# Solve products of a gated DeltaNet as units in TensorE's order, and VectorE's order at three layer ends

## The chip, the core and the metric

The kernel runs on one core of a Trainium2 chip, as one launch. The metric is the device time of that launch in microseconds (us). Before the change it is 1340.41 us, the median of 3 runs from 1339.39 to 1340.73.

## What is computed

A bidirectional encoder trunk of two layers on 512 tokens of width 1024, all in float32: first a gated DeltaNet mixer (8 heads, in chunks of 64 tokens), then a gated linear attention (GLA) mixer (4 heads), each followed by an MLP of width 4096 with squared ReLU. After each of these four parts stands a LayerNorm of the residual sum.

```python
def reference(x, ...):
    for i in range(DEPTH):                                   # 2
        m = _mixer_gdn(x, ...) if i % 2 == 0 else _mixer_gla(x, ...)
        x = _layernorm(ALPHA * x + m, ln1_g[i], ln1_b[i])
        x = _layernorm(ALPHA * x + _sq_relu_mlp(x, mlp_w1[i], mlp_w2[i]), ln2_g[i], ln2_b[i])

def _gated_delta_chunked(q, k, v, beta, g):                  # one direction, per chunk of 64
    gc = cumsum(g); kb = k * beta
    a_mat = where(strict, (kb @ k.T) * decay_mat, 0.0)
    sol = triangular_solve(a_mat + eye(64), [v * beta, kb * exp(gc)], lower, unit_diagonal)
    ...
```

What the change touches most is the triangular solve: for each head, both directions and all chunks, the inverse of a unit triangular matrix.

## The kernel before

Tokens lie in four tiles of 128 (t0 to t3, buffers xt0 to xt3). Products of float32 are done as three matmuls (lines 122 to 124) on operands split into a high and a low half: ScalarE copies the high half (names with h: wh, xth, ah), VectorE subtracts it for the low half (wl, xtl, al).

**The first mixer** (function `gdn`, class `GdnHead`) is a pipeline over heads. For each step of its loop three heads are in work: one in its recurrence (`recur`, matmuls m1, m2, m3, op), one in its solve (`solve`), one in its projections (`project`, products pjk, pjq, pjv, pjz, 24 matmuls of 512 columns each). In the last two steps pieces of the output product (oa) take the place of the projections.

**The solve** works on U = 8 units: 2 directions (d = 0, 1) x 4 tiles of 128 tokens, each tile holding two chunks. Its steps for one head:

- `ep`: the exponents of the decay, by two matmuls a direction; the second adds the causal mask (`mi`, the mask product, line 1538).
- `a4`: the 4 x 4 diagonal blocks, made on VectorE, d = 0 before d = 1. Three doubling steps (`hp`, line 1556): eight matmuls on four columns, then dc on VectorE.
- five levels s = 4, 8, 16, 32, 64 (`prod`, line 1600). Each level has the product lv<-Dd,ath, then pz made from it on VectorE (s below 32), on ScalarE (s = 32, four copies, line 1614) or on both (s = 64, lines 1628 and 1630), and then the two products lv<-pz,Xd and lv<-Xd,pz, from which VectorE updates Dd and Xd. Each product is eight matmuls u = 0 to 7; u = 0 to 3 are d = 0.
- a last correction (`nw`, lines 1646 and 1668).

**The order on each engine** is made by a scheduler from the instructions as the program traces them: an instruction is put into its engine's queue once the scheduler takes its operands to be ready, and a later one can overtake it. Two means of the kernel steer it. `in_order(engine)` chains the instructions of one engine that are traced inside it, so that they stand in the queue in that order. `issue_after(x)` keeps what is traced inside it behind x in the schedule. Neither adds a wait on the chip; there an engine runs its queue in order, and waits at the head for what isn't ready.

**The layer ends.** Behind each mixer `out_last` does the last part of the output product for tile after tile, norms it and transposes the result (`xpose`: four transposes on TensorE into tp, then xth on ScalarE and xtl on VectorE, twice a tile). The first mixer norms straight from the matmul banks (`in_ps`, `layernorm`), the second by `norm_halves`, a chain of short VectorE and ScalarE steps (lines 259 to 270) with two longer passes over the tile: the subtraction of the mean (line 263) and the affine step (line 270). An MLP's function `last` ends in the same chain for t0 and t1; `norm(2)` and `norm(3)` follow it. The next part begins with the products of the first two tiles' tokens, for which three weight blocks are split ahead (`take_ahead`); the fourth is split into ah and al at the start of `mlp`.

Of the kernel before, what the change touches and what calls it, by code (L numbers as in the profile page):

```python
# [17 lines left out]
P = 128  # L18
# [3 lines left out]
NT = S // P  # L22
# [6 lines left out]
class Ctx:  # L29
# [279 lines left out]
    def out_last(self, w, ks, lhs, z, tags, par, homes=None, xtags=("tp",), ahead=None, in_ps=True):  # L309

        nc = self.nc
        homes = iter(homes or ())
        ws = [{k: self.wrows(w, k * P, hf * 512, next(homes, None)) for k in ks[hf][::2]} for hf in range(2)]
        if ahead:
            ahead()
        if not in_ps:
            sums = [self.small.tile([P, 2], F32, name="lns", tag="lns") for t in range(NT)]
            stats = [[self.small.tile([P, 2], F32, name=f"lnv{q}", tag=f"lnv{q}") for q in range(2)] for t in range(NT)]  # L320
        pss = {}
        for t, hf in [(t, hf) for t in range(NT - 2) for hf in range(2)] + [(NT - 2, 0), (NT - 1, 0), (NT - 2, 1), (NT - 1, 1)]:
            sl = slice(t * P, (t + 1) * P)
            ps = pss[t, hf] = self.bank([P, 512], F32, name="ob", tag=tags[hf % len(tags)])
            if in_ps:
                nc.tensor.matmul(ps, self.ident, z[t][hf], start=True, stop=False)
            for i, k in enumerate(ks[hf]):
                ah, al = lhs(k, sl)
                wh, wl = ws[hf][k - i % 2]
                self.mm3(ps, ah, al, wh[:, i % 2, :], wl[:, i % 2, :], not in_ps and i == 0, i == len(ks[hf]) - 1)  # L330
            if not in_ps:
                nc.vector.scalar_tensor_tensor(z[t][hf], ps, 1.0, z[t][hf], ALU.mult, ALU.add, accum_out=sums[t][:, hf:hf + 1])
                self.half_stats(z[t][hf], sums[t][:, hf:hf + 1], stats[t][hf], ps)
            if hf:
                if in_ps:
                    self.layernorm([pss[t, 0], pss[t, 1]], self.xh(t), par)
                else:
                    self.norm_halves(z[t], par, sums[t], stats[t], (0, 1))
                if in_ps or t < NT - 2:
                    self.xpose(t, self.xt[t], xtags)  # L340
        if not in_ps:
            with self.tc.issue_after(self.normed[1].ins):
                self.xpose(NT - 2, self.xt[NT - 2], xtags)
            self.xpose(NT - 1, self.xt[NT - 1], xtags)


def mlp(c, w1, w2, g, b, out=None, extra=None):
# [8 lines left out]
    tc, nc = c.tc, c.nc  # L356
    V, A, T = nc.vector, nc.scalar, nc.tensor
# [4 lines left out]
    with c.banks(pj=2, X=2, Y=2, Z=2), tc.tile_pool(name="mlp", bufs=2) as pool:  # L362
# [5 lines left out]
        def ring(name):  # L368
            return (pool, *RING[name])
# [36 lines left out]
        def new_h():  # L406
            return [pool.tile([P, HF, S], F32, name="h", tag="h", bufs=3) for _ in range(2)]
# [192 lines left out]
        def last(gi, h, a):  # L600
# [90 lines left out]
            for j in range(2):  # L691
# [1 line left out]
            return norm, second_normed  # L693

        h = new_h()
        specs = [(c.ahead[f] if f < len(c.ahead) else c.wcols(w1, f * P, pool=ring("ah") if f == 3 else None),
                  "pj", ("pj", "pj", "X", "X")[f]) for f in range(4)]
        for f, ps in enumerate(c.proj_halves(specs)):
            act(ps, h[0][:, f, :])
# [70 lines left out]
            h, a = nh, stream.a  # L770
        with c.in_order(mybir.EngineType.PE):
            norm, normed = last(G - 1, h, a)
        norm(2)
        norm(3)
        c.normed = normed

# [123 lines left out]
class GlaHead:  # L900
# [199 lines left out]
    def norm(self):  # L1100

        c, h = self.c, self.h
        V, A, T = c.nc.vector, c.nc.scalar, c.nc.tensor
        gcol = self.consts[-1]
        rs = c.small.tile([P, NT], F32, name="rs", tag="rs")
        c.rsqrt(rs, self.ss, NT, RMS_EPS)
        for n, o in self.ob.items():
            V.scalar_tensor_tensor(o, o, rs[:, n:n + 1], self.sr[:, n, :], ALU.mult, ALU.mult)
        for i in range(2):
            ps = c.bank([P, NT, P], F32, name="otp", tag="tp")  # L1110
            for n in range(NT):
                T.transpose(ps[:, n, :], self.ob[n][:, i * P:(i + 1) * P], c.ident)
            hi = self.oth[:, 2 * h + i, :].rearrange("p (n t) -> p n t", n=NT)
            lo = self.otl[:, 2 * h + i, :].rearrange("p (n t) -> p n t", n=NT)
            A.mul(hi, ps, gcol[:, i:i + 1])
            V.scalar_tensor_tensor(lo, ps, gcol[:, i:i + 1], hi.bitcast(F32), ALU.mult, ALU.subtract)
# [260 lines left out]
class GdnHead:  # L1377
# [8 lines left out]
    def t8(self, name, bufs):  # L1386
        return self.pool.tile([P, 2 * NT, P], F16, name=name, tag=name, bufs=bufs)
# [121 lines left out]
    def solve(self, done):  # L1509

        c, pool, g, h = self.c, self.pool, self.g, self.h
        V, A, T = c.nc.vector, c.nc.scalar, c.nc.tensor
        U = 2 * NT
# [8 lines left out]
        for d in range(2):  # L1522
            ps = self.bank("ep")
# [10 lines left out]
        V.tensor_tensor(kks, kk, g.nd.unsqueeze(1).to_broadcast([P, NT, P]), ALU.mult)  # L1534
        a4 = t8("a4", 1)
        ex, ats = [], []
        for d, ps in enumerate(eps):
            T.matmul(ps, g.idb, g.mi[d].unsqueeze(1).to_broadcast([P, NT, P]), start=False, stop=True, skip_group_check=True)
            e = self.t2("E", 2)
            for n in range(NT):  # L1540
                A.activation(e[:, n, :], ps[:, n, :], AF.Exp, bias=self.cj[:, n, d:d + 1])
            at = kks if d else self.t2("on", 2)
            V.tensor_tensor(at, e, kks, ALU.mult)
            us = slice(d * NT, (d + 1) * NT)
            A.copy(ath[:, us, :], at)
            V.tensor_tensor(a4[:, us, :], ath[:, us, :], g.same4.unsqueeze(1).to_broadcast([P, NT, P]), ALU.mult)
            ex.append(e)
            ats.append(at)
# [3 lines left out]
        dc = None  # L1552
        for it in range(3):
            ps = self.bank("hp", shape=(P, U, 4))
            for u in range(U):
                T.matmul(ps[:, u, :], a4[:, u, :], g.ic if dc is None else dc[:, u, :], start=True, stop=True)
            nd = pool.tile([P, U, 4], F16, name="dc", tag="dc", bufs=2)
            V.tensor_tensor(nd, icb, ps, ALU.subtract)
            dc = nd
            if it < 2:  # L1560
                yield 0.25, 0.7
# [30 lines left out]
        def cols(t, u, s, i):  # L1592

            return t[:, u, :].rearrange("p (b two s) -> p b two s", two=2, s=s)[:, :, i ^ (u // NT), :]

        def prod(lhs, rhs, s, i):

            ps = self.bank("lv", shape=(P, U, 64 // s, s))
            for u in range(U):
                T.matmul(ps[:, u, :, :], lhs[:, u, :], cols(rhs, u, s, i), start=True, stop=True)  # L1600
            return ps.rearrange("p (d n) b s -> p d (n b) s", d=2)

        dirs = [slice(0, NT), slice(NT, U)]
# [1 line left out]
        for s in (4, 8, 16, 32):  # L1605
            pd = g.pz[s]
            ps = prod(ath, dd, s, 0)
# [9 lines left out]
            ps = prod(xd, pd, s, 0)  # L1617
# [6 lines left out]
        ps = prod(ath, dd, 64, 0)  # L1624
# [7 lines left out]
        ps = prod(xd, pd, 64, 0)  # L1632
# [8 lines left out]
        for d in range(2):  # L1641
            us = dirs[d]
            ps = self.bank("nw")
            for n in range(NT):
                u = d * NT + n
# [12 lines left out]
        for d, e in enumerate(ex):  # L1658
            t = self.t2("qke", 2)
# [3 lines left out]
        for d in range(2):  # L1663
            us = dirs[d]
            ps = self.bank("nw")
            for n in range(NT):
                u = d * NT + n
# [136 lines left out]
```

## Time and profile before

| | |
|---|---|
| median of 3 runs | 1340.41 us |
| the profiled execution: its time | 1341.23 us |
| the profiled execution: span from first to last instruction | 1339.4 us |
| mean granted clock of TensorE | 0.996 |
| instructions | 22232 |
| first mixer, by its lines | from 0 to about 425 us of the span |
| first MLP | to about 750 |
| second mixer | to about 1010 |
| second MLP | to the end |

In a row of the trace's order of time stand the start in us, the busy time in us, the engine, the line, the operation, out<-in, the shapes and a count, and in brackets the idle time in front of it and what ended that. Buffer numbers are left out there (m for m1, m2, m3). Ends of matmuls are modelled and overlap the next start, so that a matmul's busy time is longer than the distance to the next start. A float32 matmul that isn't split counts twice.

### The profile page before, as it was taken

The page shows a single profiled execution, that of the slowest core. Times are in us where ns is not written, and L with a number is a line of the kernel's source. Part 1 is how long each engine was busy: PE and PEld are TensorE (multiplying, and loading weights), DVE is VectorE, ACT ScalarE, POOL GpSimd, SP SyncE. Part 2 cuts the span into 40 slices and gives each one's busy share as a digit, 9 for nine tenths or more (in the row PEclk, how much of TensorE's full clock was granted, in tenths as well). Part 3 has the DMA queues.
Part 4 walks back from the last instruction along what each step waited for, and adds up shares of the span by engine and source line. Part 5 has one row for each costly group of instructions (what it writes and reads, how often), then busy time and mean ns, then how long its engine had stood idle before and what let it go on. Part 6 is the DMA issues. An engine that isn't in the chain of part 4 may idle for free.

```text
span 1339.4 us, 22232 instructions
## 1 busy us (share of the span) xinstructions
PE 1317.2 (98%) x8629; PEld 1124.4 (84%) x8629; DVE 1099.9 (82%) x1802; ACT 800.5 (60%) x1590; POOL 123.3 (9%) x177
## 2 busy tenths in 40 slices
PE   8999999999999999999999999999999999999996
PEld 8777878777777889999998888888889899999985
DVE  6797878788778878988988877967879678989888
ACT  4667657767643645666566754654456456565656
POOL 4000000000000910100102100000001001101011
PEclk9999999999999999999999999999999999999998
DMA  6221112112232674775748532221327475757556
GB/s 179 64 65 47 35 46 64 48 49 72 72 96 63 210 161 149 161 179 150 171 124 176 138 111 71 63 64 63 94 64 208 107 186 137 165 170 147 156 136 148
DMA packets 155660, 154.35 MB, mean 115 GB/s; under 512 B 7723, under 2 KB 122531, under 8 KB 155555
## 3 DMA queue, kind: packets, MB, share of 16 engines
q1 hardware_dynamic: 143779, 110.85, 27.8%
q0 software_dynamic: 11776, 42.08, 16.1%
q8 instruction: 68, 1.11, 0.3%
q14 instruction: 37, 0.30, 0.1%
HBM read 113.99 MB, written 2.10 MB: 87 GB/s over the span
## 4 chain that ended last, share of the span: by engine, by line
PE 86%; DVE 6%; ACT 6%; issue 1%; DMA 1%; DVEq 0%; POOL 0%; ACTq 0%; POOLq 0%
PE pX L123 3%; PE pX L122 3%; PE pX L124 3%; PE fx L124 3%; PE fx L123 3%; PE fx L122 3%; PE pjv L123 3%; PE m L1694 3%; PE pjv L122 3%; PE pjv L124 3%; PE pj L123 3%; PE pj L124 3%; PE pj L122 3%; PE fyz L124 2%; PE fyz L122 2%; PE fyz L123 2%
## 5 line engine op out<-in xcount | busy, mean ns | idle before, releaser
L101 DVE TENSOR_TENSOR wl<-wst,wh 128x1024 fp32r<-128x1024 f32 x148 | 182.3, 1232 | 49.1 <-ACT wh L96 47.8
L96 ACT CAST wh<-wst 128x1024 fp32r<-128x1024 f32 x150 | 157.7, 1051 | 101.1 <-PE fyz L123 30.1
L101 DVE TENSOR_TENSOR w2l<-w2r,w2h 128x1024 fp32r<-128x1024 f32 x92 | 112.7, 1225 | 27.2 <-ACT w2h L96 27.1
L96 ACT CAST w2h<-w2r 128x1024 fp32r<-128x1024 f32 x94 | 98.4, 1048 | 56.3 <-PE pX L124 24.8
L402 POOL DMA_DIRECT2D w2r<-w2r x56 | 48.4, 891 | 503.1 <-DVE w2l L101 290.1
L96 ACT CAST ah<-h 128x1024 fp32r<-128x1024 f32 x56 | 58.8, 1051 | 51.8 <-PE pZ L123 23.2
L451 DVE TENSOR_TENSOR wst<-wst 128x512 f32<-128x512 f32 x110 | 73.5, 688 | 0.2
L101 DVE TENSOR_TENSOR al<-h,ah 128x1024 fp32r<-128x1024 f32 x56 | 68.6, 1224 | 5.2 <-ACT ah L96 5.2
L123 PE MATMUL pX<-w2l,ah 128*128 128x512 f32 x168 | 66.1, 394 | 0.0
L122 PE MATMUL pX<-w2h,ah 128*128 128x512 f32 x168 | 66.0, 393 | 0.0
L124 PE MATMUL pX<-w2h,al 128*128 128x512 f32 x168 | 65.7, 391 | 0.0
L123 PE MATMUL pj<-xtl,wh 128*128 128x256 f32 (+1 forms) x192 | 64.6, 338 | 0.6 <-DVE xtl L188 0.6
L122 PE MATMUL pj<-xth,wh 128*128 128x256 f32 (+1 forms) x192 | 64.2, 338 | 0.3 <-ACT xth L187 0.2
L124 PE MATMUL pj<-xth,wl 128*128 128x256 f32 (+1 forms) x192 | 64.5, 337 | 0.0
L122 PE MATMUL pjv<-wh,xth 128*128 128x512 f32 x128 | 54.4, 425 | 0.0
L124 PE MATMUL pjv<-wh,xtl 128*128 128x512 f32 x128 | 50.2, 392 | 0.0
L123 PE MATMUL pjv<-wl,xth 128*128 128x512 f32 x128 | 50.0, 390 | 0.0
L124 PE MATMUL fx<-xh,wl 128*128 128x256 f32 x176 | 49.7, 283 | 0.0
L124 PE MATMUL fyz<-xh,wl 128*128 128x256 f32 x176 | 49.7, 282 | 0.0
L124 PE MATMUL fx<-xth,wl 128*128 128x256 f32 x176 | 49.7, 282 | 0.0
L123 PE MATMUL fx<-xtl,wh 128*128 128x256 f32 x176 | 49.7, 282 | 0.0
L122 PE MATMUL fyz<-xh,wh 128*128 128x256 f32 x176 | 49.7, 282 | 0.0
(528 smaller groups left out, 4319.1 us busy)
## 6 DMA issues: line engine op xcount, KB each, us to landing
wst<-in_mlp_w SPq DMA_DIRECT2D x68, 512.0 KB, 4.9
w2r<-in_mlp_w SPq DMA_DIRECT2D x60, 512.0 KB, 4.4
w2r<-w2r POOLq DMA_DIRECT2D x56, 512.0 KB, 5.6
wst<-in_a_w_in SPq DMA_DIRECT2D x32, 512.0 KB, 4.0
wst<-in_b_w_in SPq DMA_DIRECT2D x32, 256.0 KB, 3.0
wst<-in_a_w_out SPq DMA_DIRECT2D x8, 512.0 KB, 3.6
wst<-in_b_w_in SPq DMA_DIRECT2D x8, 512.0 KB, 4.2
wst<-in_b_w_out SPq DMA_DIRECT2D x8, 512.0 KB, 3.7
```

Of the source, the lines that this page charges most:

```text
L96: h = nc.scalar.copy(hi, src)
L101: self.halves = h, nc.vector.tensor_tensor(lo, src, hi.bitcast(F32), ALU.subtract)
L122: mm(ps, ah, bh, start=start, stop=False, **kw)
L123: mm(ps, ah, bl, start=False, stop=False, **kw)
L124: self.last_mm = mm(ps, al, bh, start=False, stop=stop, **kw)
L402: nc.gpsimd.dma_start(blocks[a + (q,)], blocks[b + (q,)], accum_op=ALU.add)
L451: plus = lambda a, b: V.tensor_tensor(a, a, b, ALU.add)
L1694: T.matmul(ps[:, d, :], *ops(d), start=True, stop=True)
```

## The change

In the solve, the mask products, the doubling products and the level products are each put into one chain of TensorE's order, from u = 7 down to u = 0 (d = 1 before d = 0); d = 1 is what is made last. At three layer ends, what VectorE does there is put into another order: behind the first mixer, the transposes of t2 wait in the schedule for t3's norm (as they do behind the second mixer already); at the end of the first MLP, `norm(2)` is kept behind `norm(1)`; at the start of the last MLP the split of the fourth weight block is kept behind the last transposes' halves. No arithmetic is added or left out.

```diff
@@ out_last @@
-                if in_ps or t < NT - 2:
+                if t < NT - 2:
                     self.xpose(t, self.xt[t], xtags)
-        if not in_ps:
-            with self.tc.issue_after(self.normed[1].ins):
-                self.xpose(NT - 2, self.xt[NT - 2], xtags)
-            self.xpose(NT - 1, self.xt[NT - 1], xtags)
+        with self.tc.issue_after(self.normed[1].ins):
+            self.xpose(NT - 2, self.xt[NT - 2], xtags)
+        self.xpose(NT - 1, self.xt[NT - 1], xtags)
@@ mlp @@
-        specs = [(c.ahead[f] if f < len(c.ahead) else c.wcols(w1, f * P, pool=ring("ah") if f == 3 else None),
+        specs = [(c.ahead[f] if f < len(c.ahead) else c.wcols(w1, f * P, pool=ring("ah") if f == 3 else None,
+                                                                 late=() if out is None else (c.last_hi, c.last_lo)),
                   "pj", ("pj", "pj", "X", "X")[f]) for f in range(4)]
...
             norm, normed = last(G - 1, h, a)
-        norm(2)
+        with contextlib.nullcontext() if out is not None else tc.issue_after(normed[1].ins):
+            norm(2)
         norm(3)
@@ GdnHead.solve @@
         ex, ats = [], []
+        with c.in_order(mybir.EngineType.PE):
+            for d in (1, 0):
+                T.matmul(eps[d], g.idb, g.mi[d].unsqueeze(1).to_broadcast([P, NT, P]), start=False, stop=True, skip_group_check=True)
         for d, ps in enumerate(eps):
-            T.matmul(ps, g.idb, g.mi[d].unsqueeze(1).to_broadcast([P, NT, P]), start=False, stop=True, skip_group_check=True)
             e = self.t2("E", 2)
...
             ps = self.bank("hp", shape=(P, U, 4))
-            for u in range(U):
-                T.matmul(ps[:, u, :], a4[:, u, :], g.ic if dc is None else dc[:, u, :], start=True, stop=True)
+            with c.in_order(mybir.EngineType.PE):
+                for u in reversed(range(U)):
+                    T.matmul(ps[:, u, :], a4[:, u, :], g.ic if dc is None else dc[:, u, :], start=True, stop=True)
...
             ps = self.bank("lv", shape=(P, U, 64 // s, s))
-            for u in range(U):
-                T.matmul(ps[:, u, :, :], lhs[:, u, :], cols(rhs, u, s, i), start=True, stop=True)
+            with c.in_order(mybir.EngineType.PE):
+                for u in reversed(range(U)):
+                    T.matmul(ps[:, u, :, :], lhs[:, u, :], cols(rhs, u, s, i), start=True, stop=True)
```

What the scheduler makes of it moves instructions on TensorE, VectorE, ScalarE and SP; on GpSimd nothing moves. Three places follow. Lines behind the edits have other numbers in the change (hp: 1556 before, 1560 now; m: 1694 and 1699).

TensorE, first doubling product hp of the fourth head, before (four matmuls of hp, each with its weight load, stand at each "..." and the row above it):

```order
L124 MATMUL pjq<-xth,wl 128x512
L1556 LDWEIGHTS a_2434
L1556 MATMUL hp<-icc,a_2434 128x4
...
L122 MATMUL pjq<-xth,wh 128x512
L1556 LDWEIGHTS a_2434
L1556 MATMUL hp<-icc,a_2434 128x4
...
L123 MATMUL pjq<-xtl,wh 128x512
L1694 MATMUL m_2368<-r,xf 128x128 x2
```

The same place now; at "..." stand the other seven of the eight:

```order
L123 MATMUL pjq<-xtl,wh 128x512
L1699 MATMUL m_2379<-vd,kt 128x128 x2
L1560 LDWEIGHTS a_2434
L1560 MATMUL hp<-icc,a_2434 128x4
...
L124 MATMUL pjq<-xth,wl 128x512
L122 MATMUL pjq<-xth,wh 128x512
```

Before, a projection row stood between the four products of d = 0 and those of d = 1; now all eight stand together, some rows further back. In the whole program 8 products hp and 13 products lv<-pz,Xd were cut like this and none is now; of the 8 pairs of mask products 8 were apart and 3 are.

VectorE, end of the first MLP, before. xt_5559 to xt_5562 are t0 to t3; line 625 adds a product to a tile and sums it, 263 is the pass that subtracts the mean, 270 the affine step, 188 a low half behind a transpose:

```order
L270 SCALAR_TENSOR_TENSOR xt_5559<-xt_5559,rstd,ln 128x512 x2
L198 TENSOR_TENSOR rst<-rsy 128x1
L625 SCALAR_TENSOR_TENSOR xt_5561,lns<-pX,xt_5561 128x512
L199 SCALAR_TENSOR_TENSOR rst<-bmv,rst 128x1
L259 SCALAR_TENSOR_TENSOR bmv<-lns,bias_83 128x1
L200 TENSOR_SCALAR rst<-rst 128x1
L263 SCALAR_TENSOR_TENSOR xt_5561<-xt_5561,bmv,ln 128x512
L205 TENSOR_TENSOR rstd<-rsy,rst 128x1
L188 TENSOR_TENSOR xtl<-tp,xth 128x4x128
L270 SCALAR_TENSOR_TENSOR xt_5560<-xt_5560,rstd,ln 128x512 x2
L188 TENSOR_TENSOR xtl<-tp,xth 128x4x128 x3
L263 SCALAR_TENSOR_TENSOR xt_5561<-xt_5561,bmv,ln 128x512
```

The same place now (line 625 is 624 here):

```order
L270 SCALAR_TENSOR_TENSOR xt_5559<-xt_5559,rstd,ln 128x512 x2
L198 TENSOR_TENSOR rst<-rsy 128x1
L624 SCALAR_TENSOR_TENSOR xt_5561,lns<-pX,xt_5561 128x512
L199 SCALAR_TENSOR_TENSOR rst<-bmv,rst 128x1
L200 TENSOR_SCALAR rst<-rst 128x1
L205 TENSOR_TENSOR rstd<-rsy,rst 128x1
L270 SCALAR_TENSOR_TENSOR xt_5560<-xt_5560,rstd,ln 128x512 x2
L188 TENSOR_TENSOR xtl<-tp,xth 128x4x128 x4
L624 SCALAR_TENSOR_TENSOR xt_5562,lns<-pX,xt_5562 128x512
L259 SCALAR_TENSOR_TENSOR bmv<-lns,bias_83 128x1
L264 SCALAR_TENSOR_TENSOR bmv<-lnv_8590,lnv_8591,lnt 128x1
L263 SCALAR_TENSOR_TENSOR xt_5561<-xt_5561,bmv,ln 128x512 x2
```

t1's affine step no longer stands behind t2's mean, t2's first pass and t0's first low half; both passes of t2 now stand behind all four low halves and t3's sum. TensorE's order doesn't change here.

VectorE, end of the second mixer and start of the last MLP, as a piece of the difference (xt_5562 is t3; al is the low half of the fourth weight block; w2r, line 420 before and 419 now, are sums over the tokens that the MLP needs later):

```order
 L270 SCALAR_TENSOR_TENSOR xt_5562<-xt_5562,rstd,ln_9214 128x512
-L188 TENSOR_TENSOR xtl<-tp,xth 128x4x128 x2
+L188 TENSOR_TENSOR xtl<-tp,xth 128x4x128 x4
+L419 TENSOR_TENSOR w2r<-xth,xtl 128x1024
 L101 TENSOR_TENSOR al<-wst,ah 128x1024
-L188 TENSOR_TENSOR xtl<-tp,xth 128x4x128 x2
-L420 TENSOR_TENSOR w2r<-xth,xtl 128x1024 x4
-L101 TENSOR_TENSOR w2l<-w2r,w2h 128x1024
+L419 TENSOR_TENSOR w2r<-xth,xtl 128x1024 x3
```

al stood between the two low halves of t2 and those of t3; now all four stand together, and al behind the first of the w2r sums. On ScalarE ah moves in the same way, behind the four high halves.

## Prediction

> **What bounds the kernel now.** I read the page first, then TensorE's instructions in order of time, start against start.
>
> ```profile
> PE 1317.2 (98%) x8629; PEld 1124.4 (84%) x8629; DVE 1099.9 (82%) x1802; ACT 800.5 (60%) x1590; POOL 123.3 (9%) x177
> ...
> PE 86%; DVE 6%; ACT 6%; issue 1%; DMA 1%; DVEq 0%; POOL 0%; ACTq 0%; POOLq 0%
> ...
> 100.00:200.00 100.00, 99.33 (x911) 78.92 (x911) 81.97 (x169) 62.33 (x178) 0.00 (x0) 1.00 0.16 43
> ```
>
> TensorE is busy for 98% of the span and has 86% of the chain that ended last. The third line (a stretch inside the first mixer: TensorE, weight loads, VectorE, ScalarE, GpSimd, then granted clock 1.00) shows it busy in 99.3 of 100 us while VectorE has 82. So no other engine bounds a stage by its amount of work. The change removes no matmul. It can only gain in two ways: what TensorE loses between one matmul and the next, and the short waits at its queue. "Busy" hides both, because matmul ends are modelled; I therefore subtract starts.
>
> **Part 1: units that are no longer cut.** TensorE near 180 us, two doubling products on four columns (hp) of one head:
>
> ```profile
> 179.88 0.25 PE L1556 MATMUL hp<-icc,a 128*128 128x4 f16 x4
> 180.00 0.47 PE L122 MATMUL pjq<-xth,wh 128*128 128x512 f32 x1
> 180.31 0.25 PE L1556 MATMUL hp<-icc,a 128*128 128x4 f16 x4
> 180.43 0.48 PE L123 MATMUL pjq<-xtl,wh 128*128 128x512 f32 x1
> 180.75 0.60 PE L1694 MATMUL m<-r,xf 128*128 128x128 f32 x4
> ...
> 182.45 0.34 PE L1556 MATMUL hp<-dc,a 128*128 128x4 f16 x8
> 182.66 0.48 PE L123 MATMUL pjq<-xtl,wh 128*128 128x512 f32 x1
> 182.97 0.40 PE L124 MATMUL pjq<-xth,wl 128*128 128x512 f32 x1
> 183.21 0.39 PE L122 MATMUL pjq<-xth,wh 128*128 128x512 f32 x1
> ```
>
> A projection row (pjq) that stands behind another keeps TensorE for 183.21 - 182.97 = 0.24. One that stands behind a small unit keeps it for 0.31 (180.00 to 180.31, and 182.66 to 182.97). Cut in two, eight hp and two projection rows take from 179.88 to 180.75, 0.87 us. Whole, eight hp and two projection rows take from 182.45 to 183.21, 0.76. **A cut costs 0.11 us.** In the order of before, all 8 first hp products and 13 of the 40 level products on pz are cut; in the order of the change none is. So 21 x 0.11 = 2.3 us go. Bounds: the mixed streams shift too, and the returns from anything else into 512-column rows fall only by 17 (460 to 443), so at least 17 x (0.31 - 0.24) = 1.2; at most 2.8, if the five mask products that also join count in full.
>
> By the Trainium skill, "TensorE: Matmul & The Clock Gate", section "Step-by-step: what each phase is for", weight loads are pulled ahead of matmuls in flight, so that the next weights load while the present matmul runs. Read strictly, a return would then cost nothing and this term would be zero. The 0.31 against 0.24 in the rows above does not agree.
>
> **Part 2: waits in the solve.** A product now stands in the queue until its last-made operand is there, and the rest follows without a wait. The projection rows that fill the time in front of it are more: between a level's first product (lv<-Dd,ath) and the next (lv<-pz,Xd) the order of before has three rows in 10 of 40 places, the change never fewer than four (4 or 5 in 19, 6 and more in 21). In front of nw<-Dd,ath there were two rows in 4 of 8 heads, now in 2.
>
> ```profile
> 199.24 0.39 PE L123 MATMUL pjz<-xtl,wh 128*128 128x512 f32 x1
> 199.62 0.28 PE L1600 MATMUL lv<-pz,Xd 128*128 128x64 f16 x4
> 200.17 0.28 PE L1600 MATMUL lv<-pz,Xd 128*128 128x64 f16 x4 [0.27 <-ACT pz L1614]
> ...
> L1600 PE MATMUL lv<-pz,Xd 128*128 128x64 f16 x320 | 18.8, 193 | 1.3 <-ACT pz L1614 0.5 <-ACT pz L1630 0.2
> ...
> L1646 PE MATMUL nw<-Dd,ath 128*128 128x128 f16 x64 | 8.6, 220 | 0.9 <-ACT Dd L1635 0.5
> ...
> 199.04 1.08 ACT L1614 CAST pz<-lv 32x128 f16<-32x128 f32 x4
> ```
>
> The group rows show 1.3 + 0.9 = 2.2 us of idle. More is hidden: from 199.24 to 199.62 lie 0.38, not 0.24, with no idle told. About twenty starts in the solves lie so; if each hides what a row's modelled end covers (0.39 - 0.24 = 0.15), 20 x 0.15 = 3.0 more, 5.2 in all. Not all goes. At the level of 32 four copies on ScalarE (1.08 us for the four) must now be done before the first matmul, not two of them; four rows in front are about 0.31 + 3 x 0.24 = 1.03, and so up to 0.3 stays in the heads with only four rows there. I take half, **2.5 us**. Bounds: 5.2 gone, or 1.5 more than now, if some 5 units stand 0.3 late. Behind a waiting unit stands all of TensorE's queue: the projections, whose banks ScalarE and VectorE empty, and the recurrence of the head before.
>
> **Part 3: three layer ends.** End of the first MLP (tiles t0 to t3 are normalised, transposed, and fed to the next layer):
>
> ```profile
> 748.67 0.40 PE L124 MATMUL pX<-h,al 128*128 128x512 f32 x1
> 750.07 1.32 PE L184 MATMUL tp<-ident,xt 128*128 128x128 f32 x8 [1.00 <-DVE xt L270]
> ...
> 757.50 1.23 PE L184 MATMUL tp<-ident,xt 128*128 128x128 f32 x8
> ...
> 762.85 0.34 PE L148 MATMUL gps<-xtl,wh 128*64 128x256 f32 x1 [0.26 <-DVE xtl L188]
> ...
> 747.94 0.75 DVE L263 SCALAR_TENSOR_TENSOR xt<-xt,bmv,ln 128x512 f32<-128x512 f32 x1
> ...
> 748.68 0.68 DVE L188 TENSOR_TENSOR xtl<-tp,xth 128x512 fp32r<-128x512 f32 x1
> 749.28 1.40 DVE L270 SCALAR_TENSOR_TENSOR xt<-xt,rstd,ln 128x512 f32<-128x512 f32 x2
> ...
> 756.61 1.41 DVE L270 SCALAR_TENSOR_TENSOR xt<-xt,rstd,ln 128x512 f32<-128x512 f32 x2
> ...
> 758.70 1.42 DVE L270 SCALAR_TENSOR_TENSOR xt<-xt,rstd,ln 128x512 f32<-128x512 f32 x2
> ...
> 760.83 0.63 ACT L848 ACTIVATE w2r<-w2f 32x512 fp32r<-32x512 f32 x1
> 761.48 1.07 ACT L187 CAST xth<-tp 128x512 fp32r<-128x512 f32 x2
> ```
>
> TensorE is free at 748.67 + 0.24 = 748.9 and starts the transposes of t1 at 750.07: 1.1 us lost to the affine step of t1 (749.28). From 747.94 to 749.28, 1.34 us, stand in front of it t2's first pass, one short step and t0's low half. The change takes the pass and the low half away; less some 0.2 in which the short steps then wait for each other, the affine step starts 1.1 earlier and this wait goes. But the same two instructions now stand between t1 and t2's affine step: by the same starts, the four low halves, t3's sum and four half passes put that step near 756.3, not 756.61, and t3's near 758.2, not 758.70. So the transposes at 757.50 come only 0.3 earlier, and TensorE stands there for some 0.8. The last wait, gps at 762.85, hangs on the high halves of t3 at 761.48, behind the gate weights at 760.83, which wait until t3's affine step has ended; all of that comes 0.5 earlier. So 1.1 are won and 0.6 given back: **0.5 us**, bounds 0 and 1.1.
>
> End of the second mixer: the split of a fourth MLP weight block (ah, al) is kept behind the last transposes.
>
> ```profile
> 1013.37 0.39 PE L123 MATMUL pj<-xtl,wh 128*128 128x256 f32 x1 [0.56 <-DVE xtl L188]
> ...
> 1017.07 0.28 PE L122 MATMUL pj<-xth,ah 128*128 128x256 f32 x1
> ...
> 1011.49 1.23 DVE L101 TENSOR_TENSOR al<-wst,ah 128x1024 fp32r<-128x1024 f32 x1
> 1012.63 1.28 DVE L188 TENSOR_TENSOR xtl<-tp,xth 128x512 fp32r<-128x512 f32 x2
> ...
> 1011.67 1.19 ACT L187 CAST xth<-tp 128x512 fp32r<-128x512 f32 x2 [0.22 <-PE tp L184]
> ```
>
> TensorE stands 0.56 for a low half of t3, which stood behind al (1011.49). Without al it starts when its high half is done, 1011.67 + 0.6 = 1012.25, not 1012.63: **0.4 us**, bounds 0 and 0.56. al then runs between 1014.6 and 1015.8, behind the first w2r sum, and is needed at 1017.07 - 0.4: covered by the projection rows between, with 0.9 to spare. Without that cover it would hold TensorE's rows on ah.
>
> End of the first mixer: t2's transposes are kept behind t3's norm.
>
> ```profile
> 436.28 0.28 PE L123 MATMUL pj<-xtl,ah 128*128 128x256 f32 x1
> 436.78 0.51 PE L122 MATMUL pj<-xth,wh 128*128 128x256 f32 x2 [0.21 <-ACT xth L187]
> 437.17 0.38 PE L124 MATMUL pj<-xth,al 128*128 128x256 f32 x1
> ...
> 440.29 0.28 PE L123 MATMUL pj<-xtl,wh 128*128 128x256 f32 x1
> ...
> 439.12 0.69 DVE L188 TENSOR_TENSOR xtl<-tp,xth 128x512 fp32r<-128x512 f32 x1 [1.41 <-ACT xth L187]
> ```
>
> Two rows of the second half of the tokens stand among the ah rows at 436.78 and wait for t3's high half: 436.28 to 437.17 is 0.89 for three rows of 0.12, so some 0.5 is lost; the change puts them further back, behind al, which comes forward by one low half. Against it, t3's transposes are put some ten rows of 0.12 later. Its last low half, over at 439.8 now, would be over near 441, and the rows that read it (twelve rows of 0.12 behind those that start at 440.3) come at 441.7. I take **0.3 us** won, bounds 0.5 lost and 0.5 won.
>
> **Sum.** 2.3 + 2.5 + 0.5 + 0.4 + 0.3 = 6.0 us. Against the profiled execution's 1341.23 (span 1339.4 and 1.8 around it) that is 1335.2. That execution lies 0.8 above the median of the runs, 1340.41, so I forecast 1334.4, written 1334.5. POOL's order is the same; on SP two weight loads change places with MLP blocks that are needed many us later, which I cost at nothing: the loads run ahead of VectorE and ScalarE there. If that cover were gone, one late block would cost up to its landing time, 4.9 us:
>
> ```profile
> wst<-in_mlp_w SPq DMA_DIRECT2D x68, 512.0 KB, 4.9
> ```
>
> **Rivals.**
> 1. The waits stay. A unit that waits for its last operand at the head of the queue holds up as much as two halves did; part 2 is nothing, and of part 3 half comes: 2.3 + 0.6 = 2.9, so 1337.5. For it: the 1.08 us of copies on ScalarE. Against: more rows stand in front nearly everywhere.
> 2. A cut costs nothing: the longer distance behind a unit is made up again by what follows. Then part 1 is zero and 6.0 - 2.3 = 3.7 is left, so 1336.7. The 0.87 against 0.76 over the same work speaks against it. (This is what the Trainium skill's rule above would give.)
> 3. Slower: VectorE's order, which changes through the whole first mixer, makes last operands later than the rows in front cover. All 40 products on pz then wait 0.3 each at the queue's head, 12 us, against 3.5 from parts 1 and 3: 8.5 slower, 1349. It decides where an operand takes over 1.03 us from the product before, which is four rows. Against: 82% busy VectorE has gaps, and the longer rows in front are in its favour.
> 4. All waits of part 2 go, and each end gives all it can: 2.3 + 5.2 + 1.1 + 0.56 + 0.5 = 9.7, so 1330.7.
> That the change doesn't do what it says is excluded by the orders: no unit that it names is cut any more.
>
> **How the numbers follow.** Forecast 0.60 (its own range 1332 to 1338), rival 1 0.23, rival 2 0.04, rival 3 0.06, rival 4 0.07. A measurement of this kernel can tell about 0.2%, 2.7 us: faster means under 1337.7. The forecast gives 0.56 to that and 0.04 to no change; rival 1 lies on the border, 0.11 and 0.12; rival 2 gives 0.03 and 0.01; rival 4 all of its 0.07; rival 3 is the slower side. So faster 0.77, same 0.17, slower 0.06. The range 1331 to 1339 leaves out rival 3, half of rival 4 and the forecast's and rival 1's tails, some 0.15 in all.
>
> **What would show it.** Right: hp<-icc and lv<-pz in runs of eight everywhere; fewer rows of 0.31; idle before lv<-pz and nw<-Dd,ath under half of 2.2; the transposes of t1 at the first MLP's end directly behind pX, but a new wait of some 0.8 at t2's; the wait at pj<-xtl in front of the last MLP down to about 0.15. Wrong: lv<-pz waiting in most heads; new waits in the recurrence (m, op) or at rtp and ktp; a wait at pj<-xth,ah, or at the second half of the tokens behind the first mixer.

## The result, and the profile after

| | before | after |
|---|---|---|
| median | 1340.51 us (20 runs, 1338.59 to 1341.17) | 1338.42 us (20 runs, 1336.46 to 1339.26) |
| ratio of the times | | 0.9985, 95% interval 0.9979 to 0.9991 |
| the profiled execution: its time, span | 1341.23, 1339.4 us | 1337.19, 1335.5 us |

The change makes the kernel 2.1 us faster, where 6.0 were forecast. The two profiled executions stand 4.0 us apart; 1.7 of these arise in the first 15 us, where both kernels run the same program and the clock that TensorE was granted was 0.89 in the one and 1.00 in the other (the last section shows it). So I compare stages from the first rtp product on (48.66 us before, 46.95 after).

Of the page of after, engines and chain of work, and the stretch from 100 to 200 us (columns as before):

```profile
PE 1313.2 (98%) x8629; PEld 1122.0 (84%) x8629; DVE 1097.8 (82%) x1802; ACT 800.3 (60%) x1590; POOL 124.2 (9%) x177
...
PE 87%; DVE 5%; ACT 5%; issue 1%; DMA 1%; DVEq 0%; POOL 0%; ACTq 0%; POOLq 0%
...
100.00:200.00 100.00, 98.70 (x922) 79.36 (x920) 81.88 (x171) 68.35 (x193) 0.00 (x0) 1.00 0.17 45
```

TensorE bounds the kernel as before. In the first mixer its busy share has *fallen*, from 99.33 to 98.70 of 100 us: there is more open waiting. The groups of the first mixer (20 to 405 us) say where; before they had 1.3 and 0.9 us of idle:

```profile
L1605 PE MATMUL lv<-pz,Xd 128*128 128x64 f16 x320 | 16.2, 194 | 1.7 <-ACT pz L1619 1.3
...
L1651 PE MATMUL nw<-Dd,ath 128*128 128x128 f16 x64 | 8.7, 219 | 2.0 <-ACT Dd L1640 1.8
```

The units are whole, and yet the idle told at the two places rose from 2.2 to 3.7 us. The prediction wanted it under 1.1. Since modelled ends hide a part of each wait, I also took distances between starts: of every product that follows a 512-column row between 50 and 395 us, less 0.235 us where that row follows another row and 0.315 where it follows anything else. By these the waiting at lv<-pz hardly changed (2.70 us before, 2.51 now: 14 waits became 8 longer ones), at nw<-Dd,ath it rose from 2.10 to 2.75, and in front of qk and the recurrence's m from 0.1 to 1.0. Elsewhere it fell by about 1.0; over all such products it is 6.35 before and 6.65 now. One head of after in order of time, TensorE first, then ScalarE, then VectorE:

```profile
242.86 0.41 PE L1605 MATMUL lv<-Dd,ath 128*128 128x64 f16 x8
...
245.39 0.39 PE L1605 MATMUL lv<-pz,Xd 128*128 128x64 f16 x8 [0.42 <-ACT pz L1619]
...
249.05 0.41 PE L1605 MATMUL lv<-pz,Xd 128*128 128x64 f16 x8
...
251.20 0.22 PE L1651 MATMUL nw<-Dd,ath 128*128 128x128 f16 x1 [0.22 <-ACT Dd L1640]
...
242.34 1.92 ACT L1444 ACTIVATE sil<-sil 128x2048 f32<-128x2048 f32 x1
244.28 1.06 ACT L1619 CAST pz<-lv 32x128 f16<-32x128 f32 x4
...
248.05 0.38 ACT L1635 ACTIVATE pz<-lv 64x256 f16<-64x256 f32 x1
...
249.69 1.06 ACT L96 CAST wh<-wst 128x1024 fp32r<-128x1024 f32 x1
250.78 0.76 ACT L1640 CAST Dd<-lv 64x256 f16<-64x256 f32 x2
...
248.46 0.42 DVE L1633 TENSOR_SCALAR pz<-lv 64x256 f16<-64x256 f32 x1 [0.69 <-ACT pz L1635]
```

Three readings. At the level of 32 the unit starts at 245.39, 0.05 behind the end of the fourth copy (244.28 + 1.06); the copies stood behind a step of 1.92 us in ScalarE's queue. At nw the copies of Dd stand behind a weight split of 1.06 us. At the level of 64 the unit starts at 249.05 although the later half of its operand, VectorE's, ended at 248.88 (ScalarE's at 248.43): the rows in front covered it, here by 0.2 us and in the 8 heads by 0.15 to 0.83. So in this head TensorE waits for ScalarE's *queue* at two places and not at the third. Not every wait is the queue's: in three heads at the level of 32, and in three at nw, ScalarE's copies start 0.04 us behind the modelled end of their product, and what is waited for is the copies themselves.

At nw two things came together. Over the 8 heads the second copy of Dd ends 1.51 us behind the start of the last product on pz, and before it was 1.16; and the 512-column rows between that product and nw are 17 in all, where they were 19. All 8 heads start the level of 32 just 0.05 behind the fourth copy; before, 7 of 8 started 0.5 us ahead of its end, which is 0.05 behind the second copy (one 0.3 ahead).

The three layer ends of after, in order of time:

```profile
745.89 0.40 PE L124 MATMUL pX<-h,al 128*128 128x512 f32 x1
746.16 1.32 PE L184 MATMUL tp<-ident,xt 128*128 128x128 f32 x8
...
753.29 0.28 PE L124 MATMUL pjq<-xth,wl 128*128 128x256 f32 x1
754.14 1.23 PE L184 MATMUL tp<-ident,xt 128*128 128x128 f32 x8 [0.57 <-DVE xt L270]
...
745.35 1.42 DVE L270 SCALAR_TENSOR_TENSOR xt<-xt,rstd,ln 128x512 f32<-128x512 f32 x2
...
753.25 1.42 DVE L270 SCALAR_TENSOR_TENSOR xt<-xt,rstd,ln 128x512 f32<-128x512 f32 x2
...
1009.40 0.39 PE L123 MATMUL pj<-xtl,wh 128*128 128x256 f32 x1 [0.22 <-DVE xtl L188]
...
437.17 0.28 PE L124 MATMUL pj<-xth,al 128*128 128x256 f32 x1
437.29 0.28 PE L122 MATMUL pj<-xth,wh 128*128 128x256 f32 x1
```

First MLP: t1's transposes start 0.27 behind the last pX row, not 1.40 (748.67 to 750.07 before), and t2's now wait: 753.29 + 0.12 to 754.14 is 0.73. Last MLP: the wait for t3's low half is 0.22, not 0.56. First mixer: the second half of the tokens starts behind all the ah and al rows, 0.12 after the last of them, without a wait.

What each stage takes, after minus before, from differences of TensorE's starts in the two traces and in two experiments that follow:

| stage (from one start to another) | forecast | after | ends alone | solve alone |
|---|---|---|---|---|
| first mixer: first rtp to t0's transposes | -4.8 | -0.41 | +0.23 | -0.16 |
| its end: to the first fx of the first MLP | -0.3 | -0.64 | -0.65 | +0.01 |
| end of the first MLP, to the first gps of the second mixer | -1.1 | -1.13 | -1.14 | 0.00 |
| to the last gps there | +0.6 | +0.34 | +0.35 | -0.01 |
| second mixer's end and start of the last MLP, to its first fx | -0.4 | -0.36 | -0.35 | -0.03 |

### The profile page after: what moved, and what is told of

The parts are those of the page before. It is cut to its first block, busy times and chain, and to the rows that moved or that the text cites. A ratio compares the mean times of both kernels' runs of the same rounds, so it can differ in the third digit from the quotient of the medians.

```text
span 1335.5 us, 22220 instructions
## 1 busy us (share of the span) xinstructions
PE 1313.2 (98%) x8629; PEld 1122.0 (84%) x8629; DVE 1097.8 (82%) x1802; ACT 800.3 (60%) x1590; POOL 124.2 (9%) x177
## 4 chain that ended last, share of the span: by engine, by line
PE 87%; DVE 5%; ACT 5%; issue 1%; DMA 1%; DVEq 0%; POOL 0%; ACTq 0%; POOLq 0%
PE pX L123 3%; PE pX L122 3%; PE pX L124 3%; PE fx L124 3%; PE fx L123 3%; PE fx L122 3%; PE pjv L122 3%; PE pjv L123 3%; PE pjv L124 3%; PE m L1699 3%; PE pj L123 3%; PE pj L124 3%; PE pj L122 3%; PE fyz L122 2%; PE fyz L124 2%; PE fyz L123 2%
```

## The experiments

Ten experiments ran; e8, which adds work, stands outside the table. Medians are of 11 runs (20 for the change, 5 for e5 and e10). Each ratio is to the kernel before on the same chip; the last column is the time from the first rtp to the first fx, against before, which leaves the first 48 us out.

| run | median, us | ratio, 95% interval | rtp to fx, us |
|---|---|---|---|
| the change | 1338.42 | 0.9985 (0.9979 to 0.9991) | -1.05 |
| e1 the ends alone | 1338.94 | 0.9986 (0.9978 to 0.9995) | -0.42 |
| e2 the solve alone | 1340.38 | 1.0000 (0.9991 to 1.0009) | -0.16 |
| e3 hp units alone | 1340.28 | 0.9998 (0.9988 to 1.0007) | -0.37 |
| e4 change, copies at 32 shared | 1339.94 | 0.9994 (0.9986 to 1.0003) | +0.29 |
| e5 change, copies behind 64 shared | 1333.79 | 0.9954 (0.9940 to 0.9967) | -4.46 |
| e6 change, both shared | 1343.12 | 1.0014 (1.0004 to 1.0024) | +2.57 |
| e7 change, units from u = 0 up | 1338.07 | 0.9983 (0.9974 to 0.9991) | -0.67 |
| e9 ends, copies behind 64 shared, no units | 1337.23 | 0.9982 (0.9973 to 0.9991) | -2.49 |
| e10 as e5, level of 32 in halves | 1334.54 | 0.9962 (0.9949 to 0.9974) | -4.55 |

**e1 and e2: which half of the change works.** e1 keeps the edits of `out_last`, `mlp` and `last` and takes back those of `solve`; e2 is the reverse.

> Only the three layer ends are changed; the solve is as before. Reading of the two traces by differences of starts: the ends bring 0.6 + 0.8 + 0.35 = about 1.75 us, the solve's units almost nothing (0.4). Theory W (the units win 2.3 us of cuts and lose about 2.0 again in new waits at their heads): 1.75 us faster than before, so nearly the whole of the change's 2.1. Rival U (the units bring what the change brings, and the ends give back elsewhere what they win): within 0.5 us of before.

> Only the units of the solve are changed; the layer ends are as before. Theory W: 0.4 us faster than before, by the trace 2.3 us fewer cuts and some 2.0 us more waiting in the first mixer. Rival U: about 2 us faster. The step of the prediction as it stood would give 4.8 us faster.

The ends bring 0.9986 by themselves, the solve nothing that can be measured. The table of stages shows the same: the ends' terms are those of the whole change to within 0.02 us, and the solve's column is near zero. Rival U falls. The table's first row needs care. Up to t0's transposes e1 has before's order on every engine, and e2 has the change's; so +0.23 against 0, and -0.16 against -0.41, are what two executions of one order differ by there. The four traces with the old order (before, e1, e7, e8) have a mean of 370.12 us for that row and the two with the new one 369.77: the units won some 0.35 us, with about 0.25 of scatter.

**e3: only the hp units.**

```diff
-            for u in range(U):
-                T.matmul(ps[:, u, :], a4[:, u, :], g.ic if dc is None else dc[:, u, :], start=True, stop=True)
+            with c.in_order(mybir.EngineType.PE):
+                for u in reversed(range(U)):
+                    T.matmul(ps[:, u, :], a4[:, u, :], g.ic if dc is None else dc[:, u, :], start=True, stop=True)
```

> Only the products on four columns (hp) are made units; level and mask products are as before. Their operands come from VectorE in short steps, so a unit here should hardly wait. Theory W (a cut costs 0.11 us): 8 cuts go, 0.9 us faster than before, less whatever the shifted rows uncover. Rival C (a cut costs nothing): 0. With a 95% interval of some 0.06% this is near what can be told; the trace's first mixer tells more: the sum of the distances from start to start of the projection rows behind hp.

0.9998: by time alone it can't be told from zero or from 0.9. I counted in the order of starts, between 50 and 395 us, how often a 512-column row stands behind something else. Behind hp it fell from 32 to 24, but in all only from 237 to 236: nw's rose by 5, otp's by 2. The cuts moved.

**e8: the price of a cut, by itself.** Behind the end of the kernel before, TensorE runs patterns whose operands all lie ready.

```diff
+                def unit(us, w):
+                    for u in us:
+                        nc.tensor.matmul(few[:, u, :w], idh, idh[:, :w], start=True, stop=True)
...
+                    for _ in range(24):
+                        unit(range(8), w)
+                        row(4)
...
+                    for _ in range(24):
+                        unit(range(4), w)
+                        row(2)
+                        unit(range(4, 8), w)
+                        row(2)
```

> The kernel before, and behind its end a measurement by itself on TensorE, with operands that lie ready: 24 times a unit of eight small products and four rows of 512 columns, then 24 times the same with the unit cut (four, two rows, four, two rows); once with products on 4 columns and once with products on 64. Theory W (a cut costs 0.11 us): the cut pattern takes 24 x 0.11 = 2.6 us longer than the whole one, with both widths; a row behind a unit keeps TensorE for 0.31 us, one behind a row for 0.23. Rival C (a cut costs nothing, what was seen in the kernel are waits): both patterns take the same time to 0.3 us.

The order of time of e8 (bms are the small products, 4 and then 64 columns wide, bmb the rows):

```profile
1339.97 0.35 PE L1798 MATMUL bms<-bmh 128*128 128x4 f16 x8
1340.19 1.17 PE L1794 MATMUL bmb<-xth 128*128 128x512 f32 x4
1341.20 0.35 PE L1798 MATMUL bms<-bmh 128*128 128x4 f16 x8
...
1370.11 0.25 PE L1798 MATMUL bms<-bmh 128*128 128x4 f16 x4
1370.23 0.72 PE L1794 MATMUL bmb<-xth 128*128 128x512 f32 x2
...
1371.45 0.25 PE L1798 MATMUL bms<-bmh 128*128 128x4 f16 x4
...
1403.85 0.41 PE L1798 MATMUL bms<-bmh 128*128 128x64 f16 x8
...
1406.36 0.41 PE L1798 MATMUL bms<-bmh 128*128 128x64 f16 x8
...
1436.53 0.29 PE L1798 MATMUL bms<-bmh 128*128 128x64 f16 x4
...
1439.25 0.29 PE L1798 MATMUL bms<-bmh 128*128 128x64 f16 x4
```

Eight products and four rows take 1.23 us whole (1339.97 to 1341.20) and 1.34 cut (1370.11 to 1371.45). With 64 columns two such rounds take 2.51 whole and 2.72 cut. Over all 23 rounds it is 28.22 against 30.67 us, **0.106 us a cut**, and with 64 columns 28.83 against 31.27, the same. Rival C falls, and with it the second rival of the prediction: the price of 0.11 was right. Both patterns have the same weight loads. The Trainium skill says in "TensorE: Matmul & The Clock Gate", section "Step-by-step: what each phase is for", that the next weights load while the matmul before them runs. That does not make a return free: it costs 0.106 us here. What the time goes into, e8 doesn't show.

**e7: does the order inside the unit matter?** As the change, with `range(U)` for `reversed(range(U))` and the mask products in their old order, all still chained.

> The whole change, but every unit from u = 0 up to u = 7 (what is made first stands first). Theory W (a unit costs the wait for its last operand whichever way it is run, since no row can stand inside): within 0.6 us of the change; at the level of 32 the first half starts 0.5 us earlier and the wait stands in the middle of the unit. Rival L (last-made first is what brings the gain, a wait in the middle of a unit is worse than one ahead): 1 us or more slower than the change.

The time is that of the change, and yet neither theory had the reason. One place of e7 in order of time:

```profile
199.13 0.28 PE L1605 MATMUL lv<-pz,Xd 128*128 128x64 f16 x4
199.68 0.28 PE L1605 MATMUL lv<-pz,Xd 128*128 128x64 f16 x4 [0.27 <-ACT pz L1619]
```

The units are cut in fours as before (237 returns, as in before): the chain from u = 0 up let the scheduler put rows between, the chain from u = 7 down, whose *first* link waits for the last operand, didn't. On every engine e7's instructions stand in e1's order, so e7 is e1 once more, and -0.67 against -0.42 is scatter. What a whole unit run from u = 0 up would cost stays untested.

**e4: the copies at the level of 32, two on each engine.**

```diff
-                        A.copy(pd[r0:r0 + s, dirs[d], c0:c0 + s],
+                        (V.tensor_copy if d else A.copy)(pd[r0:r0 + s, dirs[d], c0:c0 + s],
```

> The whole change, and in addition the four copies that make pz at the level of 32 are shared: two on ScalarE, two on VectorE, side by side. In the trace of the change the product on pz there starts 0.05 us behind the end of the fourth copy in all 8 heads, 0.29 to 0.59 us later than the rows in front need. Theory W (a unit waits for the last operand that ScalarE makes, so the wait is the length of its copies): the last operand comes about 0.5 us earlier, most of the 2.9 us of waiting at this place goes: 2 to 2.5 us faster than the change, about 1336. Rival Q (what makes it late is where the copies stand in the engines' queues; on VectorE they stand behind 0.7 to 1.2 us steps too): less than 0.8 us either way.

Slower than the change by 1.3 us from the first rtp to the first fx (by 1.5 in the medians, whose intervals overlap), though the waits of that place went: in all 8 heads the unit starts 0.67 us or more behind ScalarE's copies. VectorE and TensorE of e4 near 367 us:

```profile
366.83 0.39 PE L123 MATMUL oa<-wl,oh 128*128 128x512 f32 x1
368.55 0.40 PE L1605 MATMUL lv<-pz,Xd 128*128 128x64 f16 x8 [1.33 <-DVE pz L1614]
...
367.21 0.69 DVE L305 SCALAR_TENSOR_TENSOR qd<-qd,oa 128x512 f32<-128x512 f32 x1 [2.31 <-DMA qd<-in_x]
367.81 0.68 DVE L1614 TENSOR_TENSOR pz<-lv,off 128x512 f16<-128x512 f32 x1
```

In the redrawn order a sum that waits 2.31 us for a load of x stands ahead of pz in VectorE's queue; in the change the same sum has no such wait. Rival Q names the kind of cause; that the redrawing costs more than the place wins, neither had.

**e5 and e6: the copies behind the last level shared**, in e5 alone, in e6 together with e4's.

```diff
-            A.copy(dd[row(1 - d), dirs[d], row(d)], ps[row(1 - d), d, :, :])
+            (V.tensor_copy if d else A.copy)(dd[row(1 - d), dirs[d], row(d)], ps[row(1 - d), d, :, :])
         for d in range(2):
-            V.tensor_copy(xd[row(d), dirs[d], row(1 - d)], px[row(d), d, :, :])
+            (A.copy if d else V.tensor_copy)(xd[row(d), dirs[d], row(1 - d)], px[row(d), d, :, :])
```

> The whole change, and in addition the copies behind the last level are shared otherwise: the two that make Dd (0.76 us in a row on ScalarE in the change) go one to ScalarE and one to VectorE, and so do the two that make Xd. In the change the product nw<-Dd,ath starts 0.05 us behind the second copy in 6 of 8 heads and waits 2.9 us in all 8. Theory W (the wait is the length of ScalarE's copies and what stands ahead of them there): the second copy comes some 0.35 us earlier, up to 2.4 us less at this place; so 1 to 2.4 us faster than the change, if the redrawn order brings no new wait of its size. Rival Q (any wait that is taken away is given back elsewhere, since the rows that cover are a fixed number): within 0.8 us of the change, 1338.4.

> The whole change with both divisions of copies: those that make pz at the level of 32 and those behind the last level. With the first alone the waits at its place went and the first 350 us came out some 2 us shorter than in the change, and then VectorE stood 2.3 us for a load of x with pz behind it, and the end of the first mixer was some 3 us longer. Theory W: the sum of both places, 2 to 4.5 us faster than the change, if VectorE isn't held up by that load again; with it 1 to 2 us slower. Rival Q: within 0.8 us of the change.

e5 is the fastest kernel of the study, 0.9954 of before; it is 4.6 us under the change in the medians and 3.4 from the first rtp to the first fx. Groups of 20 to 405 us of e5, and the place behind the last level in the head shown above:

```profile
L1605 PE MATMUL lv<-pz,Xd 128*128 128x64 f16 x320 | 16.2, 194 | 1.1
...
L1651 PE MATMUL nw<-Dd,ath 128*128 128x128 f16 x64 | 9.0, 221 | 0.0
```

```profile
247.06 0.41 PE L1605 MATMUL lv<-pz,Xd 128*128 128x64 f16 x8
...
248.74 0.40 PE L124 MATMUL pjk<-xth,wl 128*128 128x512 f32 x1
248.98 0.23 PE L1651 MATMUL nw<-Dd,ath 128*128 128x128 f16 x1
...
247.51 0.37 ACT L1640 CAST Dd<-lv 64x256 f16<-64x256 f32 x1 [0.83 <-PE lv L1605]
...
247.18 1.21 DVE L101 TENSOR_TENSOR wl<-wst,wh 128x1024 fp32r<-128x1024 f32 x1
248.31 0.41 DVE L1640 CAST Dd<-lv 64x256 f16<-64x256 f32 x1
```

The 2.0 us of idle at nw are gone, and 0.6 at the level of 32, where ScalarE's copies now start 0.04 us behind their product's modelled end in all 8 heads (in three of the change's). Rival Q falls for this place, and more was won than theory W allowed (2.4). But it wasn't won in theory W's way. The second copy doesn't come earlier: it now stands behind a weight split of 1.21 us in VectorE's queue, and over the 8 heads it ends 1.58 us behind the start of the last product on pz, where the change has 1.51. What is new is the cover. There are 32 rows in front of nw instead of 17, four or more in 7 of 8 heads, and here nw starts 0.24 behind the last of them. So the edit won by the order that the scheduler drew for it; that two engines share the copies is not shown to be worth anything in itself.

e6 came out 9.3 us slower than e5 in the medians, against both theories; its runs lie far apart (1338.59 to 1344.31), and the profiled one is the slowest of them. Its trace loses at the end of the first mixer (from the first rtp to t0's transposes +4.13 us, e5 -2.91), where TensorE waits 1.4 us for fo and 1.0 for oh, both ScalarE's. Some 1.7 us of this is the clock's: right behind these waits, from 413.37 to 416.78 us, the granted clock is 0.50. Why the order falls out so was not followed further.

**e9: e5's copies without the units.** The edits of `solve` are taken back, e5's stay.

> The layer ends of the change and the shared copies behind the last level, but the solve's products as they were before (no units). The whole change with the shared copies took 1333.8 us. Theory W (the units win about 16 returns at 0.09 to 0.11 us, 1.4 to 1.8 us, and this showed once the wait behind the last level was gone): 1 to 2.5 us slower than that, 1335 to 1336.5. Rival N (the gain is the shared copies' alone, the units are worth nothing): within 0.6 us of 1333.8.

e9 stands at 0.9982 and e5 at 0.9954, with intervals apart; from the first rtp to the first fx they differ by 1.97 us. Without the shared copies the units were worth 0.63 there by the change against e1, and 0.16 by e2 against before. Between e9's trace and e5's the returns fall from 243 to 224, and 19 x 0.106 = 2.0. Neither has idle at nw. So the units win about what their cuts are worth where nw is covered; the other waits of the two orders differ as well, so that the sum agrees and isn't proved. Rival N falls. And e9 against e1, 2.07 us, is what the edit of the copies brings without the units.

**e10: the level of 32 in halves again**, all else as e5.

```diff
-            with c.in_order(mybir.EngineType.PE):
-                for u in reversed(range(U)):
+            whole = s != 32 or lhs is not xd
+            with c.in_order(mybir.EngineType.PE) if whole else contextlib.nullcontext():
+                for u in reversed(range(U)) if whole else range(U):
```

> The whole change with the shared copies behind the last level, and the first product on pz at the level of 32 as it was before: in two halves, with a row between. The rest of TensorE's order stays. Theory W (a cut costs 0.11 us, a wait what is uncovered): as a unit it waits until 1.34 us behind lv<-Dd,ath in all 8 heads, and lv<-Xd,pz starts at 1.58; in halves with a row between it stood at 1.47 before. So 0.1 us won in each head, 0.9 us faster, about 1333: here the cut is worth more than it costs. Rival P (the price of a cut decides): 8 x 0.11 = 0.9 us slower.

Neither: -4.55 against -4.46 from rtp to fx, the medians 0.8 apart with intervals that overlap. The same head, first in e5, then in e10:

```profile
242.28 0.41 PE L1605 MATMUL lv<-Dd,ath 128*128 128x64 f16 x8
...
244.06 0.40 PE L1605 MATMUL lv<-Xd,pz 128*128 128x64 f16 x8
...
245.15 0.39 PE L1605 MATMUL lv<-Dd,ath 128*128 128x64 f16 x8
```

```profile
243.15 0.41 PE L1606 MATMUL lv<-Dd,ath 128*128 128x64 f16 x8
...
244.83 0.40 PE L1606 MATMUL lv<-Xd,pz 128*128 128x64 f16 x8
...
246.03 0.39 PE L1606 MATMUL lv<-Dd,ath 128*128 128x64 f16 x8
...
245.22 0.16 DVE L1505 SCALAR_TENSOR_TENSOR c<-fq 128x4 f32<-128x4 f32 x1 [0.56 <-ACT fq L1504]
245.30 0.68 DVE L1625 TENSOR_TENSOR Dd<-Dd,lv 128x512 f16<-128x512 f16 x1
```

From lv<-Dd,ath to lv<-Xd,pz it is 1.78 us as a unit and 1.68 in halves, in all 8 heads: the 0.10 forecast. To the next lv<-Dd,ath it is 2.87 and 2.88: all given back, as in six of the 8 heads, since Dd's update stands in VectorE's queue behind c, which waits for a step of ScalarE, and so begins 2.14 us behind lv<-Dd,ath in e5 and 2.15 in e10. The operand's path sets the pace here, and TensorE's arrangement only chooses where it waits.

## Why the prediction was half right

- **What bounds the kernel, and the sign.** Right. The time came out on the fast side, inside the range, at a third of the forecast.
- **Part 1, the price of a cut.** Right: 0.11 forecast, 0.106 measured (e8).
- **Part 1, the number of cuts: mis-sized.** 2.3 us were 21 cuts. The named units did lose theirs: returns to rows behind lv fell by 16, behind hp by 8. But behind the recurrence's m they rose by 11, and in all they fell from 237 to 221. 16 x 0.106 = 1.7 us (1.4 with the kernel's own 0.32 against 0.23). I had read the order of the units, and used the net count only as the lower bound; it was the count to use.
- **Part 2, the waits: the step that failed.** The prediction put it: "I take half", 2.5 us. The size of what was there was right: by starts 2.7 and 2.1 us before, 4.8 where 5.2 were told. That half of it would go was wrong. At lv<-pz 0.2 went, at nw 0.65 came, and 0.9 came in front of qk and m, which the sum had at nothing (the signs of being wrong named the recurrence). By the balance of the stage some 1.0 to 1.3 us of waiting were added: from the first rtp to t0's transposes the change wins 0.41 and 1.4 to 1.7 of cuts are gone. That is near the bound told, "1.5 more than now". Only 0.3 of it is in the count behind 512-column rows; where the rest lies stays open.
- **Part 2, why.** The argument was "the projection rows that fill the time in front of it are more", with the operand coming when it came before. Both failed at nw. That there were "two rows in 4 of 8 heads, now in 2" was no gain: other heads now have one row or none, with short products in their place, and in all there are 17 rows instead of 19. And the operand came later behind its product, 1.51 us instead of 1.16, as in five heads other work stood ahead of it in ScalarE's queue. At the level of 32, "up to 0.3 stays in the heads with only four rows there" held for the three heads with four rows; the other five have five rows and wait too, since there ScalarE's copies began 0.30 to 1.02 us behind their product. At the level of 64 the cover did suffice. e5 shows that at nw cover alone is enough: with the operand no earlier (1.58) and 32 rows in front, the idle is 0.0, and 3.4 us more are won from rtp to fx, though not all at this place. Why the scheduler deals the rows so stays open.
- **First MLP's end.** Right in mechanism and place: 1.1 won, 1.13 measured; 0.6 given back, 0.34 measured, with the new wait at t2's transposes as told (0.73 for "some 0.8"). Net 0.8 for 0.5.
- **Second mixer's end.** 0.36 for 0.4.
- **First mixer's end.** 0.64 for 0.3. The wait in front of the second half went as told; the loss set against it, t3's last low half reaching its readers late, didn't come.
- **Sum.** The ends' 1.8 and the mixer's 0.4 make 2.2, the medians' 2.1. The time fell inside the range because the ends gave 1.8 instead of 1.2 and the range was wide; of the mixer's 4.8, 0.4 came. The first rival, waits that stay, named the right step and still took it as too mild (1337.5).

## What to carry to other kernels

A unit on a busy engine is worth its cuts only if its last operand is covered: read how the engine that makes that operand is queued, and count in time, not in rows, what stands in front. Filler is a fixed supply that the scheduler deals out anew at each edit, so count cuts and waits over the whole stage, never at the named places alone. When a rearrangement gives less than its parts, look for the wait that took it: here the order drawn with the shared copies (e5) made the units worth 2.0 us instead of 0.2 to 0.6. When an edit does win, look whether its own reason shows in the trace; e5's didn't.

## What the runs showed of the hardware

The clock that TensorE is granted near the start differs from one execution to the next. Columns: the stretch, busy time of TensorE, weight loads, VectorE, ScalarE, GpSimd, then the granted clock. Before (the first 15 us, and a piece of them), then after:

```profile
0.00:15.00 15.00, 11.53 (x62) 10.89 (x63) 8.04 (x22) 6.28 (x11) 5.28 (x23) 0.89 0.84 251
...
10.56:13.98 3.42, 3.42 (x19) 3.42 (x18) 0.35 (x2) 0.59 (x1) 0.00 (x0) 0.50 0.73 201
```

```profile
0.00:15.00 15.00, 11.66 (x76) 11.17 (x77) 9.56 (x24) 7.64 (x14) 5.27 (x23) 1.00 0.85 253
```

It is one piece that is slow: before has a clock of 0.50 from 10.56 to 13.98 us, and 1.00 in the pieces beside it. TensorE has no matmul from 7.67 to 9.60 us there. After has the same gap, from 7.71 to 9.51, and no such piece behind it. In the five profiled executions with 0.89 (before, e2, e6, e7, e9) the first rtp starts at 47.95 to 48.66 us, in the seven with 1.00 (after, e1, e3, e4, e5, e8, e10) at 46.17 to 47.34. Half a clock over 3.42 us is 1.7 us, the distance between before and after. The Trainium skill, in "TensorE: Matmul & The Clock Gate", section "What's actually happening", says that the window which releases the clock runs freely and doesn't start with the kernel. The traces agree in so far as the same gap has the slow piece behind it in one execution and not in another; they show nothing of the window itself. A single pair of profiles can thus differ by up to 2.5 us, more than this change's whole effect, before its first changed instruction. And a slow piece can come later: e6 has one of 3.41 us at 413.37.
